# Chunks of 400, 400 and 256 tokens from the output projection on, and a later split of the second of two alternating weight tiles

## The chip, the cores and the metric

The kernel runs on one core of a Trainium2 chip. The core has a matrix engine (TensorE, PE in the profile), which reads weights and activations from the on-chip memory (SBUF) and writes sums into banks of a second memory (PSUM), and three engines for element-wise work: VectorE (DVE), ScalarE (ACT) and GpSimd (POOL). Each runs its own list of instructions in the order in which it was written. Transfers between HBM and SBUF are issued from such lists too: here from SyncE (SP) and, for weights, from ScalarE. The metric is the time of one execution on the device, in microseconds (us); lower is better.

## The reference

One inference step of a decoder trunk on 1056 tokens (1024 of a prompt and 32 of a sample group), width 1024, all in float32. Cut to what matters here:

```python
h = rmsnorm(x, norm_mix)
q_r, k_r, v_r, z, a_r, b_r, u, gp, ga, gb = split(h @ w_in)          # 1024 -> many columns
o = gated_delta_chunked(...)                                         # 8 heads, a recurrence over the tokens
o = rmsnorm(o, gdn_norm) * silu(z)
y_a = o @ w_proj_a
y_b = (pool_mix(u, ...) * silu(gp)) @ w_proj_b
m = sigmoid(ga) * y_a + sigmoid(gb) * y_b
x = x + m @ w_out
x = x + sigmoid(rmsnorm(x, norm_ple) @ w_ple_gate) * (p @ w_ple_proj)
y = rmsnorm(x, final_norm)
```

## The kernel before

**Tiling.** Features lie on the 128 partitions, tokens along the free dimension. The 1056 tokens are cut into three chunks of `CW` = 352. Every float32 operand of a dense layer is split into a high part that the matrix engine takes in its fp32r format and a low part (`hh` and `hl` for activations, `wh` and `wl` for weights). A *chunk* of one output tile (128 features by 352 tokens) is 8 blocks of the contraction times 3 products (`wh*hh`, `wh*hl`, `wl*hh`): 24 matmuls into one PSUM bank (`chunk`, called by all layers). A weight tile `wr` is loaded by ScalarE's queue (`fetch`), cast to `wh` by ScalarE, and `wl = wr - wh` follows on GpSimd or VectorE (`split_w`; `tile_of` hands out a tile that is split).

**Stages, in the order of time.** The columns of `w_in` and, beside them, the eight heads of the recurrence in pairs (to about 1060 us); the last of those columns are the gates `ga` and `gb`; `w_proj_b`, whose input `y` is loaded back from HBM into the `hh`/`hl` tiles that the gates read before (`y_load`, 16 loads for each chunk: `hh<-yh_d`, `hl<-yl_d`); `w_proj_a`; `w_out`; `w_ple_gate`; the final norm. Where two weight tiles are used in turn, chunk by chunk, `both` does it: the last two tiles of the gates, then tiles m = 0 and 1 of `w_proj_b`. I write (m, n) for tile m and chunk n: `both` runs (0,0), (1,0), (0,1), (1,1), (0,2), (1,2).

**What a chunk of w_proj_b needs.** While the heads run only two PSUM banks (`psd`) are there for chunks. A bank comes free when VectorE has multiplied it by a gate: `gt<-gt,psd` in `ev_b`. The gate was stored to HBM earlier (`tb_d<-gt`) and is loaded back by SP into one of three buffers (`gt<-tb_d`); the product goes out by `mb_d<-gt`.

**What sets the order.** A planner (`Weave`) writes all engines' lists. It carries generators ("threads"), a model of each engine's costs and of each queue's transfers (`Queue.rate`, bytes per ns for a partition's row: it changes only when the planner believes that data has landed), and pulls the next step of a thread between two matmuls when its model says that it is due. On the chip nothing of the model is left: an engine runs its list, and semaphores hold it until data is there.

**After the heads.** `w_out` and `w_ple_gate` keep their eight tiles in SBUF (`resident`, called by `weights_step`: names `rh`, `rl`) and go chunk by chunk, eight tiles each. `norm_ple(n)` needs all eight tiles of chunk n of `w_out`, then makes the input `gh`/`gl` of `w_ple_gate`; `norm_out(n)` ends the program: for the last chunk a sum of squares, a small chain on VectorE, a matmul that broadcasts the result (`pse<-dg,cst`), and eight products and stores.

Of the kernel before, what the change touches and what calls it, by code (L numbers as in the profile page):

```python
# [234 lines left out]
def decoder_step(ctx, tc, A, O):  # L235
    nc = tc.nc
    wv = Weave()
# [8 lines left out]
    def mm(o, l, r, ns, start=True, stop=True):  # L246
        PE.matmul(o, l, r, start=start, stop=stop)  # L247
        wv.pe(ns)
# [50 lines left out]
        eng.tensor_tensor(out=lo, in0=src, in1=hi.bitcast(F32), op=ALU.subtract)  # L299

    def set_tiles(p, name):
        mk = lambda s: [[p.tile([P, CW], F32R, name=f"{name}{s}{k}_{n}", tag=f"{s}{k}_{n}") for n in range(NCH)]
                        for k in range(KT)]
        return mk("h"), mk("l")

    def drained(g, ps, ring):

# [94 lines left out]
            if step:  # L402
                yield step

    RB = CW // 4

    def rstd(sqs, bank, mk, key=None, keys=()):


        ms, rs, tm = (mk([P, 4], nm)[0:RB] for nm in ("ms", "rs", "tm"))  # L410
# [16 lines left out]
        dg = mk([P, 4, RB], "dg")[0:RB]  # L427
        V.tensor_tensor(out=dg, in0=ident[0:RB, 0:RB].unsqueeze(1).broadcast_to([RB, 4, RB]),
                        in1=rs.unsqueeze(2).broadcast_to([RB, 4, RB]), op=ALU.mult)
        yield  # L430
        bc = bank()[:, 0:CW]
        mm(bc, ones[0:RB, :], dg.rearrange("p a b -> p (a b)"), 592)
        return bc


    hhi, hlo = set_tiles(sa, "h")
    sq = kp.tile([P, 3, H * TS], F32, name="sq")
    ssz = kp.tile([P, H * TS], F32, name="ssz")
    osm = kp.tile([P, H, TS], F32, name="osm")
# [1016 lines left out]
                SY.dma_start(t[k][n].bitcast(F32), y_d[x][k][:, ns_(n)], ("y", n, x, k))  # L1456

    def both(specs, after=None):
        ws = [tile_of(n, i) for n, i, _ in specs]
        fetch()  # L1460
        for n in range(NCH):
            for (_, _, f), w in zip(specs, ws):
                f(w, n)
                if n == 0 and w is ws[0]:
                    fetch()
                if n == NCH - 1 and raws:
                    wv.run(split_w())
            if after:
                after(n)

# [2 lines left out]
    def proj_b(w, n, m):  # L1473
# [6 lines left out]
        def ev_b(n, c, o, m=m):  # L1480
# [26 lines left out]
    def heads_end():  # L1507
        hctx.close()
        so = octx.enter_context(pool("seto"))
        for l, t in zip((ohi, olo), set_tiles(so, "o")):  # L1510
            l.extend(t)
# [18 lines left out]
    psd = banks(ctx, "psd", PB)  # L1530


    mhi, mlo = set_tiles(sa, "m")
    with pool("ew", 2) as ew:
        for m in range(KT):
            ta = ew.tile([P, T], F32, name="ta2", tag="ta2")
# [16 lines left out]

    cq = ctx.enter_context(pool("outp", 2))
    pse = ctx.enter_context(pool("pse", 2, space=PSUM))
    x1 = [[cq.tile([P, CW], F32, name=f"x1{k}_{n}", bufs=1) for n in range(NCH)] for k in range(KT)]
    ct = lambda nm, bufs=2: cq.tile([P, CW], F32, name=nm, tag=nm, bufs=bufs)

    def ssum(m, sqa, src, key):
        if m == 0 or m == KT - 1 and len(sqa) > 1:  # L1560
            S.activation(sqa[m > 0], src, AF.Square)
        else:
            q = ct("sq1")
# [6 lines left out]
        return rstd(sqs, lambda: pse.tile([P, 512], F32, name="pse", tag="pse"),  # L1570
                    lambda sh, nm: cq.tile(sh, F32, name=nm, tag=nm, bufs=1), keys=keys)

    ghi, glo = [[None] * NCH for _ in range(KT)], [[None] * NCH for _ in range(KT)]

    def norm_ple(n, sqa):
        yield [("o", 0, n, m) for m in range(KT)]
        yield
        rs = yield from rnorm(sqa)
        yield
        for k in range(KT):  # L1580
            hh = ct("hh")
            V.scalar_tensor_tensor(out=hh, in0=x1[k][n], scalar=nple[:, k:k + 1], in1=rs, op0=ALU.mult, op1=ALU.mult)
            yield
            ghi[k][n] = sa.tile([P, CW], F32R, name=f"gh{k}_{n}", tag=f"h{k}_{n}")
            glo[k][n] = sa.tile([P, CW], F32R, name=f"gl{k}_{n}", tag=f"l{k}_{n}")
            S.copy(ghi[k][n], hh)
            yield
            (G if k % 2 else V).tensor_tensor(out=glo[k][n], in0=hh, in1=ghi[k][n].bitcast(F32), op=ALU.subtract)
        wv.mark("ple", n)

    def norm_out(n, sqa):
        done = [("o", 1, n, m) for m in range(KT)]
        yield done[:-1] if len(sqa) > 1 else done
        yield
        rs = yield from rnorm(sqa, done)
        yield
        last = n == NCH - 1
        for k in range(KT):
            V.scalar_tensor_tensor(out=x1[k][n], in0=x1[k][n], scalar=nfin[:, k:k + 1], in1=rs,
                                   op0=ALU.mult, op1=ALU.mult)  # L1600
            SY.dma_start(O["yT"][k][:, ns_(n)], x1[k][n])
            if not last:
                yield

# [40 lines left out]
    for n in range(NCH):  # L1645
        sqa = [ct("sqa")]
        for m in range(KT):
            s = n * KT + m
            weights_step(s)
            addend(s + 1)  # L1650

            def ev_o(n, c, o, xr=adds[s], m=m, sqa=sqa):
                V.scalar_tensor_tensor(out=x1[m][n], in0=o, scalar=0.5, in1=xr, op0=ALU.mult, op1=ALU.add)
                yield
                yield from ssum(m, sqa, x1[m][n], (0, n, m))
            chunk(held["w_out"][m], mhi, mlo, n, ev_o)
        wv.add(norm_ple(n, sqa))
    for n in range(NCH):
        wv.until(("ple", n), data=True)
        sqa = [ct("sqa")] + [ct("sqb")] * (n == NCH - 1)  # L1660
        for m in range(KT):
            s = 24 + n * KT + m
            weights_step(s)
            addend(s + 1)

            def ev_p(n, c, o, pq=adds[s], m=m, sqa=sqa):
                t, x = ct("tg"), x1[m][n]
                end = n == NCH - 1 and m == KT - 1
                w = CW // 2 if end else CW
                for a in range(0, CW, w):  # L1670
                    S.activation(t[:, a:a + w], o[:, a:a + w], AF.Tanh, scale=0.5)
                    if not end:
                        yield
                for a in range(0, CW, w):
                    V.scalar_tensor_tensor(out=pq[:, a:a + w], in0=t[:, a:a + w], scalar=1.0, in1=pq[:, a:a + w],
                                           op0=ALU.add, op1=ALU.mult)
                    V.tensor_tensor(out=x[:, a:a + w], in0=x[:, a:a + w], in1=pq[:, a:a + w], op=ALU.add)
                    if end:
                        S.activation(sqa[1][:, a:a + w], x[:, a:a + w], AF.Square)
                if end:  # L1680
                    wv.mark("o", 1, n, m)
                    return
                yield
                yield from ssum(m, sqa, x1[m][n], (1, n, m))
            if m == KT - 1:
                wv.add(norm_out(n, sqa))
            chunk(held["w_ple_gate"][m], ghi, glo, n, ev_p)
    wv.until()


# [67 lines left out]
```

## Time and profile before

| | us |
|---|---|
| median of 3 runs | 1442.55 |
| the three runs | 1441.92, 1442.55, 1444.06 |
| the profiled execution | 1443.41 |
| its span (first to last instruction) | 1441.6 |
| TensorE busy in it | 1400.9 (97%) |
| VectorE, ScalarE, GpSimd busy | 832.8, 611.2, 406.6 |

The profile is one execution, 1.8 us of which lie outside the span; it is 0.86 us above the median of the three. A timeline row gives the start, the duration, the engine, the line, the operation and its operands, how often it stands there in a row, and in brackets how long the engine was idle before it and which instruction ended that. Matmuls are pipelined: one of 352 columns shows 0.32 us, but the next begins 0.16 us after it. POOL is GpSimd, SPq is SP's queue. Lines of small functions stand for all that call them (every matmul is on line 247, every operation of VectorE, ScalarE and GpSimd on line 186), so the operands are what tells a row's place.

### The profile page before, as it was taken

To read this page: it belongs to the slowest core of one execution; us is meant where nothing else is said; L and a number is where in the kernel's file an instruction comes from. 1 tells how busy PE (TensorE), PEld (TensorE's weight loads), DVE (VectorE), ACT (ScalarE), POOL (GpSimd) and SP (SyncE) were. 2 spreads that over 40 slices of the span, in tenths; PEclk is the share of its full clock that TensorE was granted. 3 is DMA by queue.
4 is the path that set the end of the run, shared out by engine and by line. 5 is a ranking of instruction groups with operands and counts; after the bars stand their busy time and mean duration, and the time that the engine had idled before them with its cause. 6 is when DMAs were issued, how large, how long until landed. Compare 5 with 4: busy or idle time off the path is not lost.

```text
span 1441.6 us, 24421 instructions
## 1 busy us (share of the span) xinstructions
PE 1400.9 (97%) x9138; PEld 1359.4 (94%) x9138; DVE 832.8 (58%) x1810; ACT 611.2 (42%) x1612; POOL 406.6 (28%) x336
## 2 busy tenths in 40 slices
PE   8899999999999999999999999999999999999996
PEld 7799999999999999999999899999889999999996
DVE  5686666665666635437457457457464244645654
ACT  5356565555454323544454454454223122324321
POOL 3444545454121222232132132032021112315100
PEclk9899999999999999999999999999999999999998
DMA  9222232223244413752234234236538434415132
GB/s 311 72 78 94 94 104 97 96 104 123 76 135 145 136 54 104 210 176 84 66 143 132 77 124 146 65 112 222 188 122 282 139 135 147 135 46 163 43 97 88
DMA packets 106235, 178.94 MB, mean 124 GB/s; under 512 B 19260, under 2 KB 78852, under 8 KB 106116
## 3 DMA queue, kind: packets, MB, share of 16 engines
q1 hardware_dynamic: 91716, 125.99, 26.7%
q10 hardware_dynamic: 14400, 51.39, 11.5%
q8 instruction: 72, 1.18, 0.3%
q14 instruction: 47, 0.39, 0.1%
HBM read 119.92 MB, written 57.41 MB: 123 GB/s over the span
## 4 chain that ended last, share of the span: by engine, by line
PE 84%; DVE 8%; DMA 4%; ACT 2%; issue 1%; SPq 1%; POOL 0%; ACTq 0%; DVEq 0%; POOLq 0%
PE psd L247 69%; PE psg L247 5%; PE psr L247 5%; PE psg L251 2%; DMA rw<-og_d 1%; PE sr L247 1%; DVE win L186 1%; DVE big L186 1%; DMA xt<-in_xT_dram 1%; PE sg L247 1%; PE pse L247 1%; DMA gt<-tb_d 1%; DMA pp_d<-ppt 1%; DVE sg L186 1%; DMA wr<-in_w_out_dram 1%
## 5 line engine op out<-in xcount | busy, mean ns | idle before, releaser
L247 PE MATMUL psd<-hh,wh 128*128 128x352 f32 x1728 | 570.1, 330 | 5.8 <-DVE gt L186 3.4
L247 PE MATMUL psd<-hh,wl 128*128 128x352 f32 x1728 | 567.2, 328 | 0.4 <-POOL wl L186 0.4
L247 PE MATMUL psd<-hl,wh 128*128 128x352 f32 x1728 | 565.9, 327 | 0.0
L186 POOL TENSOR_TENSOR wl<-wr,wh 128x1024 fp32r<-128x1024 f32 (+1 forms) x87 | 209.9, 2412 | 612.7 <-ACT wh L186 536.2
L247 PEld LDWEIGHTS psd<-hh,wh 128*128 128x128 f32 x1728 | 326.1, 189 | 9.4 <-DVE gt L186 4.3
L247 PEld LDWEIGHTS psd<-hl,wh 128*128 128x128 f32 x1728 | 326.4, 189 | 1.8 <-issue 0.3
L247 PEld LDWEIGHTS psd<-hh,wl 128*128 128x128 f32 x1728 | 326.0, 189 | 2.2 <-POOL wl L186 0.7
L186 DVE SCALAR_TENSOR_TENSOR acc<-xr,cw,acc 128x352 f32<-128x352 f32 x144 | 108.5, 772 | 37.3 <-ACT acc L186 35.9
L186 ACT CAST wh<-wr 128x1024 fp32r<-128x1024 f32 (+1 forms) x88 | 90.6, 1030 | 40.2 <-PE psd L247 26.7
L186 POOL TENSOR_TENSOR acc<-acc,f 128x352 f32<-128x352 f32 (+1 forms) x72 | 73.6, 1028 | 120.7 <-DVE acc L186 89.1
L186 DVE SCALAR_TENSOR_TENSOR f<-f,acc 128x352 f32<-128x352 f32 (+1 forms) x72 | 68.8, 956 | 48.2 <-ACT f L186 48.2
L186 ACT ACTIVATE gt<-psd 128x352 f32<-128x352 f32 x69 | 32.3, 468 | 113.4 <-PE psd L247 88.4
L186 DVE SCALAR_TENSOR_TENSOR gt<-gt,psd 128x352 f32<-128x352 f32 x48 | 24.8, 516 | 67.0 <-ACT gt L186 30.2
L247 PE MATMUL psd<-oh,wh 128*128 128x352 f32 x192 | 62.0, 323 | 0.7 <-DVE gt L186 0.7
L247 PE MATMUL psd<-oh,wl 128*128 128x352 f32 x192 | 61.6, 321 | 0.0
L247 PE MATMUL psd<-ol,wh 128*128 128x352 f32 x192 | 61.6, 321 | 0.0
L186 ACT COPY xr<-psd 128x352 f32<-128x352 f32 (+1 forms) x96 | 33.7, 377 | 61.1 <-PE psd L247 61.1
L186 ACT ACTIVATE f<-acc 128x352 f32<-128x352 f32 (+1 forms) x72 | 36.1, 502 | 53.0 <-POOL acc L186 41.3
L186 ACT ACTIVATE junk<-psg 128x128 f32<-128x128 f32 x128 | 36.2, 283 | 41.4 <-PE psg L251 39.7
L247 PE MATMUL psd<-mh,rl 128*128 128x352 f32 x144 | 46.5, 323 | 1.1 <-POOL rl L186 1.1
L247 PE MATMUL psd<-gh,rh 128*128 128x352 f32 x144 | 46.7, 325 | 0.0
L247 PE MATMUL psd<-mh,rh 128*128 128x352 f32 x144 | 46.5, 323 | 0.0
(289 smaller groups left out, 2521.1 us busy)
## 6 DMA issues: line engine op xcount, KB each, us to landing
wr<-in_w_in_dram ACTq DMA_DIRECT2D x64, 512.0 KB, 3.6
kq_d<-f SPq DMA_DIRECT2D x16, 512.0 KB, 2.6
F<-kq_d SPq DMA_DIRECT2D x16, 512.0 KB, 4.9
xt<-in_xT_dram SPq DMA_DIRECT2D x6, 704.0 KB, 7.4
pp_d<-ppt SPq DMA_DIRECT2D x24, 176.0 KB, 6.0
yh_d<-ysh SPq DMA_DIRECT2D x24, 176.0 KB, 2.0
yl_d<-ysl SPq DMA_DIRECT2D x24, 176.0 KB, 2.6
tb_d<-gt SPq DMA_DIRECT2D x24, 176.0 KB, 3.7
```

Source lines behind the costliest of these rows:

```text
L186: return f(*a, **k)
L247: PE.matmul(o, l, r, start=start, stop=stop)
L251: PE.transpose(o, i, idn)
```

## The change

1. `set_tiles` makes one tile of 1056 tokens for each block instead of three of 352; `thirds` and `cut` slice it, so that the same memory can be cut at other places later.
2. `both`: the first tile's split is on VectorE; the second tile is split (`tile_of`) only after the first tile's first chunk is written, and the third tile's split comes after the first tile's last chunk.
3. `SY.rate` 360 becomes 320 from the last gates on.
4. From `w_out` on the chunks are `LAST`: 400, 400 and 256 tokens. `w_out` runs them in the order 0, 2, 1, `w_ple_gate` 0, 1, 2, so the 256 are the last to be finished. `norm_ple` writes its result into the slices of `mhi`/`mlo`.

```diff
 T = TP + TS
 CW = 352
+LAST = tuple(slice(a, b) for a, b in ((0, 400), (400, 800), (800, T)))
+LW = 400
...
     def set_tiles(p, name):
-        mk = lambda s: [[p.tile([P, CW], F32R, name=f"{name}{s}{k}_{n}", tag=f"{s}{k}_{n}") for n in range(NCH)]
-                        for k in range(KT)]
+        mk = lambda s: [p.tile([P, T], F32R, name=f"{name}{s}{k}", tag=f"{s}{k}") for k in range(KT)]
         return mk("h"), mk("l")
+
+    cut = lambda tiles, cols: [[t[:, c] for c in cols] for t in tiles]
+    thirds = lambda tiles: cut(tiles, [ns_(n) for n in range(NCH)])
...
     def both(specs, after=None):
-        ws = [tile_of(n, i) for n, i, _ in specs]
+        wv.run(split_w(V))
         fetch()
+        ws = []
         for n in range(NCH):
-            for (_, _, f), w in zip(specs, ws):
-                f(w, n)
-                if n == 0 and w is ws[0]:
-                    fetch()
-                if n == NCH - 1 and raws:
+            for j, (name, i, f) in enumerate(specs):
+                if n == 0:
+                    ws.append(tile_of(name, i))
+                f(ws[j], n)
+                if j == 0 and n == NCH - 1:
                     wv.run(split_w())
+            if n == 0:
+                fetch()
             if after:
                 after(n)
...
+    SY.rate = 320
     both([(name, i, lambda w, n, to=to, m=m: chunk(w, hhi, hlo, n, gate_out(gt_r.turn, m, to)))
           for name, i, to, m in gates[-2:]], y_load)
...
+    width = [c.stop - c.start for c in LAST]
+    mhi, mlo = (cut(t, LAST) for t in mset)
...
-    ghi, glo = [[None] * NCH for _ in range(KT)], [[None] * NCH for _ in range(KT)]
+    ghi, glo = mhi, mlo
...
+    steps = [(j, n, m) for j, chunks in enumerate(((0, 2, 1), (0, 1, 2))) for n in chunks for m in range(KT)]
+
     def addend(s):
 
-        if s < 48:
-            n, m = s % 24 // KT, s % KT
-            adds[s] = ct("xr2", 3)
-            SY.dma_start(adds[s], (A["xT"] if s < 24 else pp_d)[m][:, ns_(n)])
+        if s < len(steps):
+            j, n, m = steps[s]
+            adds[s] = ct("xr2", n, 3)
+            SY.dma_start(adds[s], (pp_d if j else A["xT"])[m][:, LAST[n]])
...
+        if j:
+            chunk(held["w_ple_gate"][m], ghi, glo, n, ev_p, cols=LAST[n])
+        else:
+            chunk(held["w_out"][m], mhi, mlo, n, ev_o, cols=LAST[n])
```

**What it moves.** Up to the last two gates tiles the lists of all engines are the same. Behind them they differ, most of all at the start of `w_proj_b`, where the last pair of heads begins its triangular solve (`U`, `en`, `psg`).

TensorE, from the last matmul of the gates on, before: the solve's first products (`psg<-U,U`) come first, then chunk (0,0) in bank `psd_5725` begins between them.

```order
L247 MATMUL psd_5724<-hh_2_112,wl 128x352
L247 MATMUL psg_5730<-U_5748,U_5750 128x96 [waits DVE_49]
L247 MATMUL psg_5730<-U_5748,U_5750 128x96 x3
L247 MATMUL psg_5729<-U_5748,U_5750 128x96 x4
L247 MATMUL psd_5725<-hh_0_89,wh 128x352 [waits DMAHW1_49,Activation_49]
L247 MATMUL psd_5725<-hl_0_113,wh 128x352 [waits DMAHW2_49]
L247 MATMUL psd_5725<-hh_0_89,wl 128x352 [waits Pool_49]
L247 MATMUL psd_5725<-hh_0_92,wh 128x352 [waits DMAHW3_49]
L247 MATMUL psg_5730<-U_5758,U_5757 128x96 [waits DVE_49]
```

TensorE after, at the end of chunk (1,0), which is in bank `psd_5692`: the 24 matmuls of (0,0) in `psd_5693` and 18 of (1,0) stand ahead of these rows.

```order
L249 MATMUL psd_5692<-hh_94,wl 128x352
L249 MATMUL psg_5698<-U_5716,U_5718 128x96 [waits DVE_49]
L249 MATMUL psg_5698<-U_5716,U_5718 128x96 x3
L249 MATMUL psd_5692<-hh_95,wh 128x352
...
L249 MATMUL psd_5692<-hh_96,wl 128x352
L249 MATMUL psd_5693<-hh_89,wh 128x352 [waits DMAHW5_49,DVE_49]
L249 MATMUL psd_5693<-hl_97,wh 128x352 [waits DMAHW6_49]
L249 MATMUL psd_5693<-hh_89,wl 128x352
L249 MATMUL psg_5697<-U_5716,U_5718 128x96 x4
```

Two whole chunks now stand in front of most of the solve, and the first matmul of (0,1), `psd_5693<-hh_89,wh`, which waits for VectorE (its bank's product with the gate), stands in front of the rest of it.

VectorE before: the second transposition of `U` is followed by the solve, and the first product with a gate comes 14 rows later.

```order
L186 STREAM_TRANSPOSE U_5748<-U_5754 128x1024 [waits Activation_49,Pool_49]
L186 TENSOR_TENSOR en<-psg_5730,cst 128x4x96 [waits PE_49]
L186 STREAM_TRANSPOSE U_5758<-U_5759 128x1024 [waits Activation_49,Pool_49]
L186 TENSOR_TENSOR en<-psg_5729,cst 128x4x96 [waits PE_49]
...
L186 COPY U_5754<-psg_5730 32x4x32 [waits DVE_49,PE_49]
L186 SCALAR_TENSOR_TENSOR gt_5767<-gt_5767,psd_5725 128x352 [waits DMAHW2_49,PE_49]
L186 COPY U_5759<-psg_5729 32x4x32 [waits DVE_49,PE_49]
```

VectorE after, the same place:

```order
L188 TENSOR_TENSOR wl<-wr,wh 128x1024 [waits DMAHW1_49,PE_49,Activation_49]
L188 STREAM_TRANSPOSE U_5716<-U_5722 128x1024 [waits Activation_49,Pool_49]
L188 SCALAR_TENSOR_TENSOR gt_5735<-gt_5735,psd_5693 128x352 [waits DMAHW2_49,PE_49]
L188 STREAM_TRANSPOSE U_5726<-U_5727 128x1024 [waits Activation_49,Pool_49]
L188 TENSOR_TENSOR en<-psg_5698,cst 128x4x96 [waits PE_49]
L188 SCALAR_TENSOR_TENSOR gt_5736<-gt_5736,psd_5692 128x352 [waits DMAHW3_49,PE_49]
L188 TENSOR_TENSOR en<-psg_5697,cst 128x4x96 [waits PE_49]
```

The first and second product with a gate, which wait for loads (`DMAHW`), moved ahead of the solve, and a weight split came onto VectorE's list. On SP's list the loads `gt<-tb_d` still stand behind all 48 loads of `y`, as before.

## Rows read from the trace of the kernel before

**Rows 1.** The page, part 1: busy time and share of each engine.
```profile
PE 1400.9 (97%) x9138; PEld 1359.4 (94%) x9138; DVE 832.8 (58%) x1810; ACT 611.2 (42%) x1612; POOL 406.6 (28%) x336
```

**Rows 2.** Timeline of TensorE, last gates and start of w_proj_b (columns as told above).
```profile
979.30 0.66 PE L251 MATMUL psg<-cst,F 128*128 128x128 f32 x4 [1.52 <-ACT junk L186]
979.71 0.41 PE L247 MATMUL psd<-hh,wh 128*128 128x352 f32 x1
...
1007.77 2.02 PE L247 MATMUL psg<-U,U 128*128 128x96 f32 x16 [0.62 <-DVE U L186]
1009.58 0.41 PE L247 MATMUL psd<-hh,wh 128*128 128x352 f32 x1
...
1028.33 0.49 PE L247 MATMUL psr<-U,U 128*128 128x128 f32 x2 [1.60 <-DVE U L186]
```

**Rows 3.** Timeline of SP's queue, from the first load of y to the gates' loads.
```profile
986.36 0.49 SPq L231 DMA_DIRECT2D hh<-yh_d  x1
...
996.12 0.42 SPq L231 DMA_DIRECT2D hl<-yl_d  x1
...
1001.92 2.74 SPq L231 DMA_DIRECT2D hl<-yl_d  x1
...
1009.03 0.42 SPq L231 DMA_DIRECT2D hl<-yl_d  x1
...
1010.50 0.42 SPq L231 DMA_DIRECT2D hh<-yh_d  x1
...
1021.98 0.42 SPq L231 DMA_DIRECT2D hl<-yl_d  x1
1022.45 2.74 SPq L231 DMA_DIRECT2D gt<-tb_d  x3
```

**Rows 4.** Timeline of VectorE at the first product with a gate.
```profile
1027.56 0.52 DVE L186 SCALAR_TENSOR_TENSOR gt<-gt,psd 128x352 f32<-128x352 f32 x1 [4.29 <-DMA gt<-tb_d]
```

**Rows 5.** Windows: stretch, its length, each engine's busy us (instructions), PEclk, DMA share, GB/s.
```profile
1010.00:1015.00 5.00, 4.62 (x39) 4.08 (x39) 2.81 (x5) 0.45 (x1) 2.37 (x1) 1.00 0.97 338
...
1067.40:1070.50 3.10, 0.40 (x3) 0.11 (x1) 3.03 (x5) 0.00 (x0) 2.23 (x1) 1.00 0.01 3
1070.50:1074.00 3.50, 3.46 (x13) 3.40 (x14) 1.89 (x8) 0.00 (x0) 2.04 (x2) 0.53 0.69 201
```

**Rows 6.** Timeline of GpSimd: the low part of one weight tile.
```profile
1067.28 2.35 POOL L186 TENSOR_TENSOR wl<-wr,wh 128x1024 fp32r<-128x1024 f32 x1
```

**Rows 7.** Timeline of VectorE: the heads' last small operations, 128x8 each, and a gate's product.
```profile
1061.39 0.17 DVE L186 SCALAR_TENSOR_TENSOR os_t<-os_t,os_x 128x8 f32<-128x8 f32 x1
...
1067.38 2.27 DVE L186 TENSOR_TENSOR os_t<-os_r 128x8 f32<-128x8 f32 x1
...
1069.97 0.52 DVE L186 SCALAR_TENSOR_TENSOR gt<-gt,psd 128x352 f32<-128x352 f32 x1
```

**Rows 8.** Timeline of TensorE: matmuls of 256 and 352 columns, and two waits.
```profile
966.82 1.02 PE L247 MATMUL psg<-F 128*128 128x256 f32 x4
967.49 0.51 PE L247 MATMUL psd<-hh,wl 128*128 128x352 f32 x1
...
1070.54 0.54 PE L247 MATMUL psd<-hh,wh 128*128 128x352 f32 x1 [2.74 <-DVE gt L186]
...
1233.11 0.32 PE L247 MATMUL psd<-mh,wh 128*128 128x352 f32 x1
...
1240.89 0.32 PE L247 MATMUL psd<-mh,rh 128*128 128x352 f32 x1
...
1246.27 0.43 PE L247 MATMUL psd<-mh,rl 128*128 128x352 f32 x1 [1.09 <-POOL rl L186]
```

**Rows 9.** Timeline of TensorE at the program's end: the broadcast of the last norm.
```profile
1432.98 1.51 PE L247 MATMUL pse<-dg,cst 88*128 88x352 f32 x2 [2.82 <-DVE dg L186]
```

**Rows 10.** Timeline of VectorE there: a half of the last tile, and the last products.
```profile
1428.63 0.34 DVE L186 TENSOR_TENSOR x<-x,xr 128x176 f32<-128x176 f32 x1
...
1434.53 4.02 DVE L186 SCALAR_TENSOR_TENSOR x<-x,vec,pse 128x352 f32<-128x352 f32 x8 [1.70 <-PE pse L247]
```

More of the change, by code (lines that the diff above doesn't have):

```diff
@@ L403, in rsqrt_steps @@
                 yield step
-    RB = CW // 4
     def rstd(sqs, bank, mk, key=None, keys=()):
+        W = sqs[0].shape[1]
+        RB = W // 4
         ms, rs, tm = (mk([P, 4], nm)[0:RB] for nm in ("ms", "rs", "tm"))
@@ L426, in rstd @@
         yield from rsqrt_steps(rs, ms, tm, 0 if key else 100)
-        dg = mk([P, 4, RB], "dg")[0:RB]
-        V.tensor_tensor(out=dg, in0=ident[0:RB, 0:RB].unsqueeze(1).broadcast_to([RB, 4, RB]),
+        dg = mk([P, CW if key else LW], "dg")[0:RB, 0:W]
+        V.tensor_tensor(out=dg.rearrange("p (a b) -> p a b", a=4), in0=ident[0:RB, 0:RB].unsqueeze(1).broadcast_to([RB, 4, RB]),
                         in1=rs.unsqueeze(2).broadcast_to([RB, 4, RB]), op=ALU.mult)
         yield
-        bc = bank()[:, 0:CW]
-        mm(bc, ones[0:RB, :], dg.rearrange("p a b -> p (a b)"), 592)
+        bc = bank()[:, 0:W]
+        mm(bc, ones[0:RB, :], dg, 1.68 * W)
         return bc
-    hhi, hlo = set_tiles(sa, "h")
+    hhi, hlo = map(thirds, set_tiles(sa, "h"))
     sq = kp.tile([P, 3, H * TS], F32, name="sq")
@@ L1530, in decoder_step @@
     psd = banks(ctx, "psd", PB)
-    mhi, mlo = set_tiles(sa, "m")
+    mset = set_tiles(sa, "m")
+    mhi, mlo = map(thirds, mset)
     with pool("ew", 2) as ew:
@@ L1555, in decoder_step @@
     pse = ctx.enter_context(pool("pse", 2, space=PSUM))
-    x1 = [[cq.tile([P, CW], F32, name=f"x1{k}_{n}", bufs=1) for n in range(NCH)] for k in range(KT)]
-    ct = lambda nm, bufs=2: cq.tile([P, CW], F32, name=nm, tag=nm, bufs=bufs)
+    width = [c.stop - c.start for c in LAST]
+    mhi, mlo = (cut(t, LAST) for t in mset)
+    x1 = [[cq.tile([P, w], F32, name=f"x1{k}_{n}", bufs=1) for n, w in enumerate(width)] for k in range(KT)]
+    ct = lambda nm, n, bufs=2: cq.tile([P, LW], F32, name=nm, tag=nm, bufs=bufs)[:, 0:width[n]]
     def ssum(m, sqa, src, key):
@@ L1580, in norm_ple @@
         for k in range(KT):
-            hh = ct("hh")
+            hh = ct("hh", n)
             V.scalar_tensor_tensor(out=hh, in0=x1[k][n], scalar=nple[:, k:k + 1], in1=rs, op0=ALU.mult, op1=ALU.mult)
             yield
-            ghi[k][n] = sa.tile([P, CW], F32R, name=f"gh{k}_{n}", tag=f"h{k}_{n}")
-            glo[k][n] = sa.tile([P, CW], F32R, name=f"gl{k}_{n}", tag=f"l{k}_{n}")
             S.copy(ghi[k][n], hh)
@@ L1635, in decoder_step @@
     adds = {}
+    steps = [(j, n, m) for j, chunks in enumerate(((0, 2, 1), (0, 1, 2))) for n in chunks for m in range(KT)]
     def addend(s):
-        if s < 48:
-            n, m = s % 24 // KT, s % KT
-            adds[s] = ct("xr2", 3)
-            SY.dma_start(adds[s], (A["xT"] if s < 24 else pp_d)[m][:, ns_(n)])
+        if s < len(steps):
+            j, n, m = steps[s]
+            adds[s] = ct("xr2", n, 3)
+            SY.dma_start(adds[s], (pp_d if j else A["xT"])[m][:, LAST[n]])
     addend(0)
[L1645 to L1679, printed above, removed]
-                if end:
[L1681 to L1684, printed above, removed]
@@ new lines, in decoder_step, with ev_o, ev_p @@
+    for s, (j, n, m) in enumerate(steps):
+        last = j and n == NCH - 1
+        if m == 0:
+            if j:
+                wv.until(("ple", n), data=True)
+            sqa = [ct("sqa", n)] + [ct("sqb", n)] * last
+        weights_step(s)
+        addend(s + 1)
+        def ev_o(n, c, o, xr=adds[s], m=m, sqa=sqa):
+            V.scalar_tensor_tensor(out=x1[m][n], in0=o, scalar=0.5, in1=xr, op0=ALU.mult, op1=ALU.add)
+            yield
+            yield from ssum(m, sqa, x1[m][n], (0, n, m))
+        def ev_p(n, c, o, pq=adds[s], m=m, sqa=sqa):
+            t, x, cw = ct("tg", n), x1[m][n], width[n]
+            end = n == NCH - 1 and m == KT - 1
+            w = cw // 2 if end else cw
+            for a in range(0, cw, w):
+                S.activation(t[:, a:a + w], o[:, a:a + w], AF.Tanh, scale=0.5)
+                if not end:
+                    yield
+            for a in range(0, cw, w):
+                V.scalar_tensor_tensor(out=pq[:, a:a + w], in0=t[:, a:a + w], scalar=1.0, in1=pq[:, a:a + w],
+                                       op0=ALU.add, op1=ALU.mult)
+                V.tensor_tensor(out=x[:, a:a + w], in0=x[:, a:a + w], in1=pq[:, a:a + w], op=ALU.add)
+                if end:
+                    S.activation(sqa[1][:, a:a + w], x[:, a:a + w], AF.Square)
+            if end:
+                wv.mark("o", 1, n, m)
+                return
+            yield
+            yield from ssum(m, sqa, x1[m][n], (1, n, m))
+        if j and m == KT - 1:
+            wv.add(norm_out(n, sqa))
+        if j:
+            chunk(held["w_ple_gate"][m], ghi, glo, n, ev_p, cols=LAST[n])
+        else:
+            chunk(held["w_out"][m], mhi, mlo, n, ev_o, cols=LAST[n])
@@ L1685, in decoder_step @@
             if m == KT - 1:
-                wv.add(norm_out(n, sqa))
-            chunk(held["w_ple_gate"][m], ghi, glo, n, ev_p)
+                wv.add(norm_ple(n, sqa))
     wv.until()
```

6 lines of the change are left out of this document (3 added, 3 removed).

## Prediction

> **What bounds the kernel now.** I read the page's busy times first. TensorE is busy 97% of the span [rows 1], so 1400.9 us are matmuls that the change neither adds to nor takes from: the count stays, and 400 + 400 + 256 columns are the same 1056. What can move is the remaining 40 us of waits, the clock behind a wait, and the end of the program, where TensorE has hardly anything left. So I then read TensorE's timeline for rows with an idle time in brackets, and for each the timeline of the engine named there. Five places are touched:
>
> - the last gates: 1.52 us of idle at 979.30, where products of the heads (`psg<-cst,F`) wait for ScalarE with chunk (0,0) queued behind them [rows 2];
> - the start of w_proj_b: 0.62 us at 1007.77 and 1.60 us at 1028.33 [rows 2]. The second is the interesting one: VectorE stood idle for 4.29 us until the first gate was back from HBM [rows 4], with the solve's copies queued behind it. Its load was issued only at 1022.45, behind the last load of y [rows 3];
> - the heads' last small operations: one of a series of 0.17 us takes 2.27 us, at 1067.38 [rows 7], beside a split of 2.35 us on GpSimd that began at 1067.28 [rows 6]. A gate's product is late behind them, TensorE idles 2.74 us [rows 8], and the next 3.5 us have a granted clock of 0.53, near the 1.2 GHz level, where it had been 1.00 [rows 5];
> - w_out: 1.09 us for the low part of its fourth tile, 13 us into the stage [rows 8];
> - the tail, from 1428 us on: VectorE and a few matmuls in a chain [rows 9, 10].
>
> **The start of w_proj_b, the largest term.** Splitting the second tile late puts both chunks (0,0) and (1,0), 48 matmuls, ahead of nearly all of the solve. A matmul of 352 columns costs 0.16 us (two chunks, 48 matmuls, lie between 1233.11 and 1240.89 [rows 8]), a chunk 3.85, so 48 are 7.7 us done early. But there are two banks, and (0,1) needs the first of them emptied by a gate's product, which needs the gate's load, and that is still behind 48 loads of y. In before the solve and the 42 matmuls beside it filled the time until that load; now TensorE has done its matmuls by then and the solve is queued behind the waiting instruction, on TensorE (behind the matmul of (0,1)) and on VectorE (behind the product with the gate), so nothing else runs.
>
> When does TensorE get there? The idle of 1.52 us at 979.30 goes: in before the plan waits there for the second tile's split, and four products of the heads, which wait for ScalarE, come ahead of (0,0); without that wait they stand nine matmuls behind its start. The last gates then end some 1.5 us before the 1007.1 of before (1007.77 less 0.62 [rows 2]), at 1005.6; 7.7 us of matmuls and a few of the solve's later it is about 1013.6.
>
> When does the load land? In before it landed just before 1027.56 [rows 4]. Worst: SP's whole queue moves up by those 1.5 us and no more, 1026.0. Best: the queue isn't held for 2.74 us as at 1001.92, and the 16 loads of the last chunk of y go at the pace of the ten before 1009.45, from 1004.66 on, 0.48 each [rows 3]: issue from 1010.5 - 1.5 - 2.7 = 1006.3, 16 x 0.48 = 7.7, and 4.5 to land: 1018.5. In between: the hold stays, and the loads go at the pace of the first chunk, 16 in 10.2 us (986.36 to 996.54): 1009.0 + 10.2 + 4.5 = 1023.7. In before those 16 took 11.9 us (1010.50 to 1022.40) [rows 3] with the DMA engines 97% busy at 338 GB/s [rows 5], and the same two weight tiles are loaded beside them now, so I take the middle: 1023.3. TensorE then waits about 10 us.
>
> What is that worth? What TensorE has left behind the waiting matmul is what it had left in before at 1009.58, less the 7.7 us done early, less the wait of 1.60 that lay there, plus 1.0 for the half of the solve's first products (2.02 in all [rows 2]) that now come later: its place in before's time is 1009.6 + 7.7 + 1.6 - 1.0 = 1017.9. It restarts 0.7 us after the load: a product of 0.52 [rows 4] and the way to TensorE. So a load that lands at 1017.2 would leave the time as it is; each us later costs one. At 1023.3 that is **+6.1** (bounds +1.3 and +8.8).
>
> After such a wait I expect the lower clock, as at 1070.5: 3.5 us at 0.53 lose 1.6. The wait of 1.60 at 1028.33 had no such sequel, that of 2.74 had, so: **+1.6** (0 to 3.2). The Trainium skill, "TensorE: Matmul & The Clock Gate", section "HAM oscillation — how this bites in real kernels", says of bursts of matmuls that stand between waits for a DMA that the gate throws each next burst back to the lower clock. It speaks against this change; the trace at 1070.54 agrees. By a reading in which one wait is harmless the sum would be 1.6 lower.
>
> **The heads' last operations.** In after, the tile whose split stood between the two pairs of GpSimd's `U` products is split earlier, on VectorE, and no split stands there any more. The hold of 2.27 at 1067.38 goes: I take **-2.0** of the 2.74 (0 to -2.7), and **-1.6** for the lower clock behind it (0 to -1.6). Both would be lost if the later heads bring another split there. In "SBUF — State Buffer", section "SBUF: two separate sides", the Trainium skill tells of a port pair that VectorE with two SBUF inputs and GpSimd hold by turns, whole instructions long; rows 7 and 6 agree. By that rule the new splits on VectorE could hold up GpSimd in the same way, which has little to do there: a term of 0.
>
> **w_out.** The wait of 1.09 comes in the fourth tile, after three chunks. Chunks of 400 take 400/352 of 3.85, 4.37 each, so three give 1.57 us more: the wait is hidden, **-1.1**. The loads that follow have more time still. Running 0, 2, 1 lets norm_ple of the second 400 end while the first 400 of w_ple_gate run (8 x 4.37 = 35 us), so nothing is expected there.
>
> **The tail.** It runs at 256 instead of 352 columns. VectorE: 0.52 for 352 columns [rows 4] and 0.34 for 176 [rows 10] are 1.0 ns a column, so 96 columns fewer are 0.1 each. Eight last products: -0.8; the diagonal `dg` that feeds the broadcast: -0.1; the broadcast in its two passes, 1.51 at the lower clock [rows 9], in proportion -0.4; the halved tanh, products and square of the last tile, in all some 280 columns fewer on the path: -0.3. Together **-1.6** (-1.2 to -1.8).
>
> **Matmuls of 256 columns.** In proportion to columns they take 0.116, and the sum is unchanged: 0 is taken. Nearest rows: four of 128 columns in 0.41 [rows 2], 0.10 each, so a line to 0.16 gives 0.135 at 256; four of 256 columns in plain float32 took 0.67 [rows 8], 0.167 each. With 400 in proportion and 256 on the line, 384 matmuls cost 0.019 more each: +7; by the other kind +20. Those rows are of another number format, and small matmuls between others, so I don't take them; they are rival C. The contiguous tiles change no wait in the lists: 0.
>
> **Sum.** 6.1 + 1.6 - 2.0 - 1.6 - 1.1 - 1.6 = +1.4 on the profiled execution's 1443.41, which is 1444.8; that execution lay 0.86 above the median of the runs, so in their terms **1444.0**. A difference of 0.2% (2.9 us) is about what a measurement of this kernel can tell from none; this is within it, and the parts before and behind w_proj_a cancel.
>
> **Rivals.**
> - A, **the gates' loads come soon enough.** For it: six chunks of the gates end earlier, and y's loads need only them. Against: the DMA engines are 97% busy. At 1018.5, with no lower clock: 1.3 - 2.0 - 1.6 - 1.1 - 1.6 = -5.0, 1437.6.
> - B, slower: **the new wait in full.** The queue moves up by no more than 1.5 us: +8.8 and the lower clock, 1446.7 if the hold at 1067.38 goes, 1450.3 if it stays. It decides from a landing at about 1024.8 on (+7.6 instead of +6.1), or from 1021.2 where the hold stays. For it: the loads' pace in before was set by bytes.
> - C, slower: **256 columns off the proportion**: +7, 1451.0.
> - D, **the new order of w_proj_b is without effect**, since the bank and the load bind in either order: only w_out and the tail remain, -2.7, 1439.8.
>
> **How the numbers follow.** Forecast 40% (its own range 1440.5 to 1445.4), A 28%, B 22%, C 6%, D 4%. Faster by over 0.2% (below 1439.7): A and half of D, 0.30. Slower (above 1445.4): B and C, 0.28. Within: 0.42. For 8 in 10 the range leaves out the far halves of A, B and C: 1437.0 to 1449.0.
>
> **What would show it.** TensorE idle before the first matmul of (0,1), some 10 us, ended by a product with a gate that waited for `gt<-tb_d`; a granted clock near a half behind it; 128x8 operations on VectorE at 0.17 without the 2.27; no wait for `rl` in w_out; eight last products at 0.40 instead of 0.50; a chunk of 400 at 4.37 and one of 256 at 2.80. The forecast is wrong if that first wait is under 6 us or over 12, or if 256 columns take over 0.125.

## The result and the profile after

The changed kernel takes 1450.61 us (median of 6 runs, 1448.85 to 1453.95), against 1441.91 us of the kernel before on the same chip (6 runs, 1439.23 to 1444.06): a ratio of 1.006, 95% interval 1.0047 to 1.0073. It is slower by some 8.7 us. The profiled execution took 1453.95 us with a span of 1451.9, 10.3 us more than the span of before; both profiled executions are slower than their medians, by 3.3 and 1.5 us, so the differences below add up to 1.6 us more than that of the medians.

The page's busy times, as in [rows 1]:

```profile
PE 1405.6 (97%) x9138; PEld 1363.9 (94%) x9138; DVE 821.1 (57%) x1812; ACT 613.0 (42%) x1612; POOL 401.3 (28%) x334
```

TensorE is busy 4.7 us more with the same 9138 instructions, and waits make up the rest of the 10.3 us. Two waits stand out, each with a lower clock behind it.

The first wait is the one that was forecast. These are rows of TensorE's timeline at the start of w_proj_b and at the end of it (start, duration, operands, idle time before and what ended it), where [rows 2] and [rows 8] showed 1.60 and 2.74 us:

```profile
1010.56 0.43 PE L249 MATMUL psd<-hh,wl 128*128 128x352 f32 x1 [0.51 <-DVE wl L188]
...
1024.90 0.66 PE L249 MATMUL psd<-hh,wh 128*128 128x352 f32 x1 [9.64 <-DVE gt L188]
...
1084.49 0.40 PE L249 MATMUL psd<-hh,wh 128*128 128x352 f32 x1 [1.41 <-DVE os_t L188]
...
1129.78 0.43 PE L249 MATMUL psd<-hh,wh 128*128 128x352 f32 x1 [0.22 <-DVE gt L188]
...
1137.25 0.63 PE L249 MATMUL psd<-hh,wh 128*128 128x352 f32 x1 [3.38 <-ACT wh L188]
...
1152.25 0.40 PE L249 MATMUL psd<-oh,wh 128*128 128x352 f32 x1 [0.70 <-DVE gt L188]
```

The same two places of before, the chunk in front of w_proj_b's last tile and the start of w_proj_a:

```profile
1125.11 0.32 PE L247 MATMUL psd<-hh,wh 128*128 128x352 f32 x1
...
1141.30 0.40 PE L247 MATMUL psd<-oh,wh 128*128 128x352 f32 x1 [0.71 <-DVE gt L186]
```

The row at 1024.90 is the first matmul of (0,1), which waited 9.64 us. The row at 1152.25 is the first matmul of w_proj_a, which stood at 1141.30 before: 10.95 us later. So all of the loss, and a little more, lies ahead of w_proj_a. (0.50 us of it is older than the change: the last group of the heads' matmuls that both kernels have ahead of the changed order begins at 975.95, in before at 975.45.) The row at 1137.25 is the second place: 3.38 us of idle in front of w_proj_b's last tile, where before had none.

What the first wait hangs on is in the lists of VectorE and of SP (the answers to [rows 4] and [rows 3]):

```profile
1010.90 1.25 DVE L188 STREAM_TRANSPOSE U<-U 128x1024 f32<-128x1024 f32 x1 [0.40 <-ACT U L188]
1024.33 0.52 DVE L188 SCALAR_TENSOR_TENSOR gt<-gt,psd 128x352 f32<-128x352 f32 x1 [12.18 <-DMA gt<-tb_d]
1024.77 1.24 DVE L188 STREAM_TRANSPOSE U<-U 128x1024 f32<-128x1024 f32 x1
```

```profile
1008.57 0.36 SPq L233 DMA_DIRECT2D hh<-yh_d  x1
...
1020.57 0.42 SPq L233 DMA_DIRECT2D hl<-yl_d  x1
1021.04 1.37 SPq L233 DMA_DIRECT2D gt<-tb_d  x3
```

VectorE stood for 12.18 us at the product with the gate, with the solve's next step (the transposition of `U`) right behind it. The load of the gate was issued at 1021.04, after the last of y's loads, 1.4 us earlier than in before, and landed about 1024.2.

Windows show the clock behind each of the two waits, as [rows 5] did (stretch, length, busy us and instructions of each engine, granted clock, DMA share, GB/s):

```profile
1015.00:1020.00 5.00, 0.27 (x2) 0.00 (x0) 0.00 (x0) 0.00 (x0) 0.00 (x0) 1.00 0.96 331
1020.00:1025.00 5.00, 0.10 (x1) 0.10 (x1) 0.67 (x2) 0.00 (x0) 0.00 (x0) 0.50 0.76 235
1025.00:1030.00 5.00, 5.00 (x22) 5.00 (x23) 2.89 (x5) 0.00 (x0) 0.00 (x0) 0.50 0.36 119
1030.00:1035.00 5.00, 5.00 (x47) 4.74 (x46) 2.32 (x5) 0.00 (x0) 0.00 (x0) 0.97 0.10 30
...
1137.00:1140.00 3.00, 2.75 (x9) 2.78 (x10) 0.54 (x2) 0.23 (x1) 2.37 (x1) 0.50 1.02 415
1140.00:1145.00 5.00, 5.00 (x24) 5.00 (x24) 0.52 (x1) 0.00 (x0) 0.00 (x0) 0.71 0.74 253
```

Between 1015 and 1020 nothing computes but the end of the last matmuls (0.27 us), while the DMA engines are 96% busy; TensorE starts again at the 1.2 GHz level and gets 22 matmuls done between 1025 and 1030, against 47 in the five us behind (of several sizes in both). The second wait has the same sequel from 1137 on.

The second wait is on VectorE's list again:

```profile
1129.63 1.29 DVE L188 TENSOR_TENSOR ol<-rw,oh 128x320 fp32r<-128x320 f32 x3
1134.88 0.49 DVE L188 TENSOR_TENSOR ol<-rw,oh 128x320 fp32r<-128x320 f32 x1 [3.95 <-ACT oh L188]
1136.19 0.49 DVE L188 TENSOR_TENSOR ol<-rw,oh 128x320 fp32r<-128x320 f32 x1 [0.81 <-ACT oh L188]
1136.59 0.95 DVE L188 SCALAR_TENSOR_TENSOR gt<-gt,psd 128x352 f32<-128x352 f32 x2
```

`reload` brings the heads' outputs back from HBM (`rw<-og_d`), casts them on ScalarE (`oh`) and makes their low part on VectorE (`ol`). Two such operations waited for the reload, 3.95 and 0.81 us, and two products with gates that empty both banks stood behind them. In before the last `ol` were done at 1120.8, with six products with gates, two whole tiles of w_proj_b, still to come:

```profile
1119.85 0.91 DVE L186 TENSOR_TENSOR ol<-rw,oh 128x320 fp32r<-128x320 f32 x2 [0.29 <-ACT oh L186]
1121.43 0.52 DVE L186 SCALAR_TENSOR_TENSOR gt<-gt,psd 128x352 f32<-128x352 f32 x1 [0.67 <-PE psd L247]
```

TensorE's row names ScalarE's cast of a weight tile as the releaser, because that cast, begun at 1136.19, ended last; but counted in their order, the cast of w_proj_b's last tile is the one before (at 1129.79), and this is w_proj_a's first tile, which TensorE did not need yet. The experiment with `ol` on GpSimd below shows which of the two it was.

The tail and the last two layers:

```profile
1440.11 1.11 PE L249 MATMUL pse<-cst,sqb 128*64 128x1 f32 x8 [1.42 <-ACT sqb L188]
1443.90 1.19 PE L249 MATMUL pse<-dg,cst 64*128 64x256 f32 x2 [2.67 <-DVE dg L188]
```

```profile
1445.12 3.22 DVE L188 SCALAR_TENSOR_TENSOR x<-x,vec,pse 128x256 f32<-128x256 f32 x8 [1.37 <-PE pse L249]
```

The eight last products take 3.22 instead of 4.02 us [rows 10], the broadcast 1.19 instead of 1.51 [rows 9]. From the last dense matmul (1438.41, before 1426.86) to the end of the span it is 13.5 us instead of 14.7. No row waits for `rl` any more. From w_out's first matmul to the last dense matmul it is 194.5 us (1243.90 to 1438.41), before 193.75 (1233.11 to 1426.86).

### The profile page after: what moved, and what is told of

It reads as the page before. It is cut to its first block, busy times and chain, and to the rows that moved or that the text cites. A ratio compares the mean times of both kernels' runs of the same rounds, so it can differ in the third digit from the quotient of the medians.

```text
span 1451.9 us, 24423 instructions
## 1 busy us (share of the span) xinstructions
PE 1405.6 (97%) x9138; PEld 1363.9 (94%) x9138; DVE 821.1 (57%) x1812; ACT 613.0 (42%) x1612; POOL 401.3 (28%) x334
## 4 chain that ended last, share of the span: by engine, by line
PE 85%; DVE 7%; DMA 4%; ACT 2%; issue 1%; SPq 0%; ACTq 0%; POOL 0%; DVEq 0%
PE psd L249 71%; PE psg L249 5%; PE psr L249 5%; PE psg L253 2%; PE sr L249 1%; DVE win L188 1%; DMA rw<-og_d 1%; DVE big L188 1%; DMA hl<-yl_d 1%; PE sg L249 1%; PE pse L249 1%; DMA xt<-in_xT_dram 1%; DMA pp_d<-ppt 1%; DMA out_delta_s_dram<-sg 1%; DVE sqs L188 1%
## 5 line engine op out<-in xcount | busy, mean ns | idle before, releaser
L188 POOL TENSOR_TENSOR wl<-wr,wh 128x1024 fp32r<-128x1024 f32 (+1 forms) x85 | 205.3, 2415 | 609.7 <-ACT wh L188 488.6
L249 PEld LDWEIGHTS psd<-hh,wh 128*128 128x128 f32 x1728 | 327.1, 189 | 22.0 <-DVE gt L188 10.4
L249 PE MATMUL psd<-mh,rl 128*128 128x400 f32 (+1 forms) x288 | 93.6, 325 | 0.0
L249 PE MATMUL psd<-ml,rh 128*128 128x400 f32 (+1 forms) x288 | 93.2, 324 | 0.0
L249 PE MATMUL psd<-mh,rh 128*128 128x400 f32 (+1 forms) x288 | 92.9, 323 | 0.0
L249 PEld LDWEIGHTS psd<-mh,rh 128*128 128x128 f32 x288 | 54.2, 188 | 0.3
```

The lines of the kernel that those rows point to most:

```text
L188: return f(*a, **k)
```

## The experiments

**Theories.** Theory 1: the loss is the new order at the start of w_proj_b, through two waits: the first for the gate's load behind y, the second for `ol` on VectorE's list. Theory 2: the widths carry it, by matmuls of 256 columns. The experiments take the change apart, and then take away what each wait hangs on.

Each experiment gives its own measurement of the kernel before, on the same chip; the changed kernel was not run beside them, so two kernels are compared by their ratios to before.

**The widths alone.** The changed kernel with `both` as in before and without the change of the rate.

```diff
     def both(specs, after=None):
-        wv.run(split_w(V))
+        ws = [tile_of(n, i) for n, i, _ in specs]
         fetch()
...
-    SY.rate = 320
```

> The changed kernel with both() and SY.rate as in before: contiguous tiles and the widths 400, 400, 256 alone. Theory 1 (the loss is the new order at the start of w_proj_b and what follows from it): no wait of 9.6 us near 1015-1025, w_proj_a begins near 1141 as in before; behind it -1.1 for the wait for rl, -1.3 in the tail, +1.9 for matmuls a little over proportion to their columns: 0 to -2 us against before. Theory 2 (the widths carry the loss): +4 us or more, with matmuls of 256 columns at over 0.125 us.

Measured: 1439.27 us against 1442.19, ratio 0.9984 (0.9972 to 0.9996). Theory 2 falls; the widths (with the contiguous tiles) are worth a gain of about 2 us. In the changed kernel's timeline a matmul of 256 columns begins 0.118 us after the one before it, one of 400 columns 0.182. The two rows below, of groups of TensorE's instructions by shape, are of this kernel: shapes, count, busy us, mean ns of one. (That mean is the duration of a pipelined matmul, longer than the distance to the next.)

```profile
L249 PE MATMUL psd<-mh,rl 128*128 128x400 f32 x192 | 66.3, 345 | 0.0
...
L249 PE MATMUL psd<-mh,rl 128*128 128x256 f32 x96 | 27.2, 283 | 0.0
```

**The order alone.** The changed kernel with chunks of 352.

```diff
-LAST = tuple(slice(a, b) for a, b in ((0, 400), (400, 800), (800, T)))
-LW = 400
+LAST = tuple(slice(a, b) for a, b in ((0, 352), (352, 704), (704, T)))
+LW = 352
...
-    steps = [(j, n, m) for j, chunks in enumerate(((0, 2, 1), (0, 1, 2))) for n in chunks for m in range(KT)]
+    steps = [(j, n, m) for j, chunks in enumerate(((0, 1, 2), (0, 1, 2))) for n in chunks for m in range(KT)]
```

> The changed kernel with the chunks of the last two layers back at 352, 352, 352 in the order 0, 1, 2: both(), SY.rate and contiguous tiles alone. Theory 1: the wait of some 10 us ended by the first product with a gate stays, and w_proj_a begins 7 to 11 us later than in before: +7 to +11 us. Theory 2: within 3 us of before.

Measured: 1451.34 against 1442.19, ratio 1.0069 (1.0048 to 1.0089). Its profile has both waits, 9.24 and 3.29 us, and w_proj_a begins at 1147.59. The whole loss is in this part.

**The gates' loads first.** One edit of the changed kernel: two loads move ahead of y's last sixteen. (In the trace the first stands ahead of all of them, the second, at 1010.54, behind two.)

```diff
+    def gates_back(n):
+        if n == NCH - 1:
+            for m in range(2):
+                pre.append(gt_r.turn())
+                SY.dma_start(pre[-1], tb_d[m][:, ns_(0)])
+        y_load(n)
...
-          for name, i, to, m in gates[-2:]], y_load)
+          for name, i, to, m in gates[-2:]], gates_back)
...
-        tb = gt_r.turn()
-        SY.dma_start(tb, tb_d[m][:, ns_(n)])
-        tbs.append(tb)
+        if pre:
+            tbs.append(pre.pop(0))
+        else:
+            tbs.append(gt_r.turn())
+            SY.dma_start(tbs[-1], tb_d[m][:, ns_(n)])
```

> The changed kernel with one edit: the loads of the first two gates of w_proj_b (chunk 0 of m = 0 and 1) are issued on SP ahead of the last 16 loads of y instead of behind them. Theory 1: the load lands some 9 to 12 us earlier, the wait of 9.6 us in front of (0,1) shrinks to under 2 us, the lower clock behind it goes, and the time falls by 8 to 12 us to 1439-1443. If the wait was set by something else than that load (the loads of y themselves, or the solve), it stays above 5 us and the time above 1447.

Measured: 1439.25 against 1442.19, ratio 0.9982 (0.9968 to 0.9997). Against the changed kernel's 1.006 that is 0.78%, 11 us, by two loads that were moved; TensorE's list keeps the order of the changed kernel around the wait. SP, VectorE and TensorE in its trace:

```profile
1008.15 0.39 SPq L233 DMA_DIRECT2D gt<-tb_d  x1
...
1013.57 0.52 DVE L188 SCALAR_TENSOR_TENSOR gt<-gt,psd 128x352 f32<-128x352 f32 x1 [1.70 <-DMA gt<-tb_d]
...
1124.36 0.40 PE L249 MATMUL psd<-hh,wh 128*128 128x352 f32 x1 [3.38 <-ACT wh L188]
```

The gate's product is at 1013.57, TensorE has no wait there of more than 0.7 us, and the granted clock from 977 to 1141 is 0.99 instead of 0.95. So of the 11 us the wait of 9.64 is the larger part, which leaves some 2 us for the slow clock behind it. The second wait is still there, and of the same 3.38 us, although everything now comes 13 us earlier: it isn't a sequel of the first wait but stands in the new order by itself.

**`ol` on GpSimd.** One edit of the changed kernel.

```diff
-        V.tensor_tensor(out=olo[k][n][:, 0:w], in0=rw[:, 0:w], in1=ohi[k][n][:, 0:w].bitcast(F32), op=ALU.subtract)
+        G.tensor_tensor(out=olo[k][n][:, 0:w], in0=rw[:, 0:w], in1=ohi[k][n][:, 0:w].bitcast(F32), op=ALU.subtract)
```

> The changed kernel with one edit: the low parts of the reloaded head outputs (ol<-rw,oh) are made on GpSimd instead of VectorE. In the changed kernel two products with gates stood behind such operations, which waited for the reload, and TensorE idled 3.4 us at 1137, with the lower clock behind it. If that queueing is the cause of this second wait, it goes, and the time falls by 3 to 6 us to 1445-1448, with the first wait of 9.6 us unchanged. If the second wait is the late load of the gates themselves, it stays: 1449-1452. If GpSimd gets late with w_proj_a's splits: slower than the changed kernel.

Measured: 1444.74 against 1442.19, ratio 1.0026 (1.0012 to 1.0039), 0.34% or 5 us below the changed kernel's. TensorE's timeline has the first wait (9.47 us), and none between 1100 and w_proj_a, which begins at 1141.80:

```profile
1022.40 0.66 PE L249 MATMUL psd<-hh,wh 128*128 128x352 f32 x1 [9.47 <-DVE gt L188]
...
1141.80 0.40 PE L249 MATMUL psd<-oh,wh 128*128 128x352 f32 x1 [0.72 <-DVE gt L188]
```

The cast of w_proj_a's first tile, named as the releaser in the changed kernel, stands here at 1129.51:

```profile
1129.51 1.05 ACT L188 CAST wh<-wr 128x1024 fp32r<-128x1024 f32 x1 [0.58 <-PE psd L249]
```

By then w_proj_b's last tile had begun, at 1129.47, and the cast ended 1.1 us later. So TensorE doesn't wait for it: the releaser was the product with the gate behind `ol`.

**Both edits.** The two edits above together.

> The changed kernel with both edits that were tried apart: the first two gates' loads ahead of the last loads of y, and ol on GpSimd. If the two waits (9.6 us at 1024.90, 3.4 us at 1137.25) are the whole of the loss and add up, both are gone and the time is 1432 to 1436. If the second wait only moves to another place once the first is gone, 1438 to 1441.

Measured: 1433.68 against 1440.47, ratio 0.9951 (0.9934 to 0.9968). That is faster than both kernels, and the two gains add up: 0.78% and 0.34% apart, 1.09% (16 us) together. Ahead of w_proj_a, TensorE's last waits are small (0.48, 1.39 and 0.71 us); the granted clock is 1.00 (a window from 977 to 1132, columns as above):

```profile
977.00:1132.00 155.00, 152.64 (x1064) 148.15 (x1062) 75.08 (x197) 48.69 (x153) 46.00 (x38) 1.00 0.66 219
```

**Both edits in the old order.** With `both` and the rate as in before, and the widths of the change.

> The same two edits and the widths 400, 400, 256, but with both() and SY.rate as in before: the order of the solve and of the first chunks of w_proj_b is that of before. If the later split is worth something once the gates' loads are in time (idle of 1.5 us in the gates, 0.6 us at the solve, 2.7 us and the lower clock at 1067-1074), this is slower than the kernel with the later split and the same edits by 3 to 6 us: 1436 to 1440. If the later split is worth nothing by itself, the two are within 2 us.

Measured: 1438.65 against 1440.47, ratio 0.998 (0.9966 to 0.9994). The two edits are worth next to nothing in the old order (0.9984 with the widths alone): there the solve's work covers most of the wait for the gates' load, and `ol` is done before the last two tiles. But the old order keeps its own waits, and with the edits the new one is 5 us better (1433.68 against 1438.65, on the same chip; the slowest of its five runs, 1433.91, is below the fastest of these ten, 1436.17). In TensorE's timeline of this kernel the waits of [rows 2] and [rows 8] are all there but two: the one for `rl` and the one at 1028.33, which the widths alone, without the edits, do not show either:

```profile
978.48 0.66 PE L253 MATMUL psg<-cst,F 128*128 128x128 f32 x4 [1.54 <-ACT junk L188]
...
1067.86 0.43 PE L249 MATMUL psd<-hh,wh 128*128 128x352 f32 x1 [2.72 <-DVE gt L188]
```

**Without the rate.** The changed kernel without `SY.rate = 320`.

```diff
-    SY.rate = 320
```

> The changed kernel without the line SY.rate = 320, so that the planner believes all loads of y and gates to land earlier. The list of TensorE then has the solve's products in a row, with no matmuls of chunks between them. If the planner's belief decides (its order is what holds TensorE), the first wait stays near 9.6 us and the solve behind it runs with TensorE idle between its steps: 1453 to 1460. If the number is without effect on the chip: 1449 to 1452.

Measured: 1447.32 against 1440.47, ratio 1.0046 (1.0028 to 1.0063), neither of the two cases. The waits in the bare solve came (0.74, 0.65, 0.51 us), behind a first wait of 9.84, which now ends at a step of the solve:

```profile
1026.82 2.02 PE L249 MATMUL psg<-U,U 128*128 128x96 f32 x8 [9.84 <-DVE en L188]
1029.59 1.56 PE L249 MATMUL psg<-U,en 128*96 128x96 f32 x8 [0.74 <-DVE en L188]
...
1035.45 2.85 PE L249 MATMUL psg<-U,en 128*64 128x64 f32 x32 [0.65 <-DVE U L188]
```

What had been left out is the second wait, which does not arise. That isn't because the reload comes sooner: its first load is at 1100.83, with 12 of w_proj_b's 24 products with gates done by then, against 1099.41 and the same 12 in the changed kernel. VectorE still waits for the reload at the end, but in this list one product alone stands behind that `ol`:

```profile
1134.77 0.52 DVE L188 SCALAR_TENSOR_TENSOR gt<-gt,psd 128x352 f32<-128x352 f32 x1
1139.03 0.49 DVE L188 TENSOR_TENSOR ol<-rw,oh 128x320 fp32r<-128x320 f32 x1 [3.74 <-ACT oh L188]
1139.44 0.52 DVE L188 SCALAR_TENSOR_TENSOR gt<-gt,psd 128x352 f32<-128x352 f32 x1
```

The product at 1134.77 had emptied the other bank, and TensorE has no idle time until w_proj_a. So a late reload makes the second wait only where both products stand behind it. The time itself tells little: the interval overlaps that of the changed kernel (1.0047 to 1.0073). It was tried with both edits too:

> The kernel with both edits (gates' loads first, ol on GpSimd) and without SY.rate = 320: TensorE's list has the solve in a row, with few matmuls of chunks between its steps. In the changed kernel leaving the line out gave 3 us back, because the second wait did not arise. If with both waits mended only the bare solve is left of its effect (waits of 0.5 to 0.8 us between its steps, and one in front of it), it is 2 to 6 us slower than the same kernel at 320: 1436 to 1440. If that order is better in itself: 1431 or less.

Measured: 1435.63 against 1441.07, ratio 0.9954 (0.9937 to 0.9971), which can't be told from 0.9951 with the rate at 320; it lies between the two cases. Its trace keeps the waits of the bare solve (0.66, 0.74, 0.65 and 0.51 us). So the planner's belief about the queue changes the lists and the waits, but these runs do not show that it is worth anything in time.

**The split on GpSimd.** The changed kernel with the first tile's split in `both` on GpSimd again.

```diff
-        wv.run(split_w(V))
+        wv.run(split_w())
         fetch()
         ws = []
```

> The changed kernel with the first tile's split in both() back on GpSimd. TensorE's list then has 95 instead of 110 matmuls of chunks between the same two groups of the solve, so more of the solve stands ahead of the matmul that waits for the gate. If the wait is the late load with too little work ahead of it, it shrinks by some 2 us: 1446 to 1449. If VectorE's split was the gain of the change and GpSimd's is later, slower than the changed kernel.

Measured: 1451.55 against 1440.47, ratio 1.0076 (1.0051 to 1.0102): as slow as the changed kernel. The wait for the gate is 8.84 us instead of 9.64, less of a gain than the 2 us expected, and TensorE now waits for the slower split in front of it:

```profile
1011.70 0.43 PE L249 MATMUL psd<-hh,wl 128*128 128x352 f32 x1 [1.89 <-POOL wl L188]
...
1024.37 2.02 PE L249 MATMUL psg<-U,U 128*128 128x96 f32 x8 [8.84 <-DVE U L188]
```

Besides the 1.89 us there are 0.94 at 1009.22, and the second wait is there with 2.37 us. So another engine for the split does not mend the start of w_proj_b; but as the edit moves both the order and the split's end, it does not weigh the two.

**The widths with both edits.** The kernel with both edits and chunks of 352.

> The kernel with both edits and the last two layers' chunks at 352, 352, 352 instead of 400, 400, 256. From the profiles of the widths alone (w_out and w_ple_gate 0.6 us longer, tail 1.2 us shorter) and the wait for rl of 1 us, which is in that 0.6: 0 to 2 us slower than with 400, 400, 256. If the widths matter more with less waiting ahead of them: over 3 us slower.

Measured: 1434.91 against 1441.07, ratio 0.9962 (0.995 to 0.9975). 0.9951 with 400, 400, 256 is a little lower, as the 0.16% of the widths alone would have it, but the intervals overlap.

## Why the prediction was wrong

1444.0 us was forecast, with a range to 1449.0; measured were 1450.6. Going through its steps with the profiled execution, whose span grew by 10.3 us:

- **The first wait: right, in its size by some luck.** The landing was taken at 1023.3, called the middle, though the middle of the bounds given, 1018.5 and 1026.0, is 1022.3; it came at about 1024.2. TensorE came to the wait at 1015.3 instead of 1013.6. Both were later than forecast, so the wait that was to be about 10 us was 9.64, ended by the product with the gate, with the solve queued behind it on both engines. "Each us later costs one" makes 7.0 of the forecast's +6.1; counted in idle time it is +6.1 (9.64 and 0.51, for the 1.52, 0.62, 0.32 and 1.60 that before had there).
- **The lower clock behind it: right, a little small.** +1.6 was taken. The clock was 0.50 from the restart to 1030, where 22 matmuls were done in five us against 47 in the next five: 5.1 us at half the clock lose some 2.5 us.
- **The heads' last operations: right, in part by another way.** The hold of 2.27 us at the second series is gone, and so is the lower clock there; the wait of 2.74 became 1.41. One hold of 2.35 us remains, in the first series, where before had one of 2.41; the list of [rows 7] in the changed kernel shows it:

```profile
1077.60 2.35 DVE L188 SCALAR_TENSOR_TENSOR os_r<-os_t,os_r 128x8 f32<-128x8 f32 x1
```

  Up to this point the forecast was +4.1 (6.1 + 1.6 - 2.0 - 1.6). The chunk that starts at 1129.78 in the changed kernel starts at 1125.11 in before: +4.7, of which 0.5 is older than the change. That this is near +4.1 is in part luck: the terms as they came out, 7.0 + 2.5 - 1.3 - 1.6, would make 6.6, and what gave the difference back wasn't found.
- **Missing: a second wait, +6.3 us.** Between that chunk and w_proj_a (+10.95) the profiled execution loses 3.38 us of idle and nearly 3 of clock. The prediction had no term for it. It followed the moved work to the `os` operations and stopped there. But with 48 matmuls done early, the heads end two chunks later against the chunks of w_proj_b: 16 of its 24 products with gates are left behind the last `os` operation, where before had 18. What the heads' end triggers, the reload `rw`, `oh` and `ol`, begins with 12 products left instead of 15 and reaches into the last tiles, where it is queued ahead of the gates' products on VectorE. This is the step that failed: what comes late next was asked once, at the wait, and not for the work that the heads release, so this wait stood at nothing in the sum. Neither sign of being wrong that it named came (a first wait under 6 or over 12 us, 256 columns over 0.125): the loss lay where it had no sign. Two experiments show it: with `ol` on GpSimd the wait is gone and 5 us with it, by the ratios; with the gates' loads first it stays, though the first wait is gone. Without it the kernel stands 0.26% above before (0.12 to 0.39), where the forecast was 0.1%. The kernel without the rate shows that a late reload alone is not enough: there VectorE's list put one product behind it, and TensorE did not wait. That the 48 matmuls are what moved the reload is read from these counts; no run tests it by itself.
- **w_out: the wait went, the gain did not come.** -1.1 was forecast for the wait for `rl`, and no such wait is left. Yet the two layers take 0.8 us more, not 1.1 less. Matmuls of 256 columns stand at 0.118 us apart, where 0.116 is in proportion: 384 of them are 0.7 us. Where the other 1.2 us went wasn't found. So this term was mis-sized by 1.9 us, which alone would have left the time within the range.
- **The tail: right in kind, 1.2 instead of 1.6.** The eight products (-0.8) and the broadcast (-0.3) came as forecast; the last tile's halves gave less than 0.3.

The sum of the terms as they came out is 4.7 + 6.3 - 0.2 (w_proj_a) + 0.8 - 1.2 = 10.4, against the span's 10.3.

Among the rivals, B ended on the right side and names a number near the result (1450.3), but for another reason: its hold at 1067.38 did go, and the landing, at about 1024.2, came ahead of the 1024.8 from which it was to decide. C is refuted by the widths alone, D by the wait itself, and A's condition, loads that come in time, did not arise; when it was made by an edit, the time was 1439.25. That this is near A's 1437.6 is luck, since that kernel still has the second wait, which A did not know; with both waits gone it was 1433.68.

## What to carry to other kernels

Work that is moved ahead of a wait must be weighed by what it was covering: here the old order hid a load behind a chain of small steps, and pulling the large work forward left the load with no cover. Then ask the same of the other end: whatever the delayed work releases is later too, and on an engine that runs its list in order it may stand in front of something that is needed. The first wait was cured in the queue: two transfers that are needed first were issued behind sixteen that are needed later. The second was cured by moving small operations to another engine's list. With both cures the new order, which had lost 8.7 us, was 5 us better than the old one with the same cures: a loss measured for a reordering can be that of the waits that it uncovers.

## What the runs showed of the hardware

Two loads of 176 KB moved ahead of y's last sixteen were worth 11 us of a program in which TensorE is 97% busy. The first of them took some 5.4 us to land there (issued 1008.15, product at 1013.57, in the kernel with the gates' loads first), with the DMA engines fully busy and the first 32 loads of y ahead of it; issued behind all 48, it took 3.3 us in the changed kernel (1021.04, product at 1024.33).

A releaser in the trace can be wrong by coincidence: ScalarE's cast ended 0.13 us after the product that did release the bank, in the changed kernel and in the one with the gates' loads first alike, since both waited for the same reload. Only a kernel in which the two came apart told which it was.
